# W loaded in two parts behind the first rows, block 0 loaded in four parts, the first store behind chunk 15

## The chip, the cores and the metric

The kernel runs on one core of a Trainium2 chip. The metric is the device time of one execution in microseconds (us). A core has the engines PE (TensorE, the matrix products), DVE (VectorE), ACT (ScalarE), POOL (GpSimd) and SP (SyncE, which here only issues transfers and waits), and 16 DMA engines that move data between HBM, the memory outside the core, and SBUF, the memory inside it. PE writes its results to PSUM, and another engine copies them from there. Engines run on their own and wait for each other by semaphores.

## The reference

```python
W_adapted = W + scale * (lora_A @ lora_B)
W_norm = np.sqrt(np.sum(W_adapted ** 2, axis=0, keepdims=True) + 1e-8)
W_final = W_adapted / W_norm * m
y = x.reshape(-1, 256) @ W_final          # x: 16 x 2048 x 256, float32
```

W is 256 x 256, lora_A 256 x 16, lora_B 16 x 256, m 256 numbers, scale 1. x has 32,768 rows of 256 numbers, which are 33.55 MB; y is as large. W is 0.26 MB.

## The kernel before

The 32,768 rows are cut into 8 blocks of 4096 rows (`NBLK`, `BLK`); each block is one SBUF buffer of 128 partitions x 32 rows, 32 KB in a partition. A block has 8 chunks (`CH`), and a chunk is 4 rows of each partition, 4 KB in a partition. Two chunks are a pair; there are 64 chunks (`NCH`) and 32 pairs (`NPR`). Five block buffers (`XBUFS`) are there for 8 blocks. Results are written over the rows that they come from, and stored from the same buffer. So a load of block 5, 6 or 7 has to wait until the store of block 0, 1 or 2 has landed (lines 148 to 152).

SP issues the loads in the order of the list `loads` (lines 110 and 111): first all of W, then block 0 in two parts (chunks 0 and 1, then the six others), blocks 1 to 6 whole, block 7 in two halves. ACT issues lora_A, lora_B and m at its start (lines 143 to 147), and the stores later, between its copies. SP's transfers are queue q1 in the profile, ACT's are q10.

The weights are made first. PE transposes lora_A (L248) and multiplies it by lora_B (L252); DVE adds W (L198, the only one that waits for W) and squares (L202); PE sums the squares over the partitions (L259) and spreads m (L264); ACT takes the root (L227); DVE multiplies by m, inverts the norm, and scales (L207 to L213), which gives `w_final`.

Then comes the stream over the pairs. POOL rounds a pair of chunks to bf16 (L176, `xb`); the first of these also waits for DVE's squares (line 173), and POOL waits for a load only where a pair is the first one of it (line 168). PE transposes the pair (L278, `xt_ps`), DVE copies that to SBUF (L217, `xt`), PE multiplies it by `w_final` (L292, `y_ps`, one half of the pair after the other), ACT copies each chunk's result into the block buffer (L234) and issues the stores. PE's order is written out by hand: the transposes of pair 0, a wait for `w_final` (line 303), and then a loop whose body is: transposes of pair p + 1, product of pair p. The product of a pair thus stands behind the transposes of the next one.

When a store is issued is set by one line and a constant, `HOLD`, 13 before:

```python
issue = [max(g0 + cnt - 1, HOLD + n) for n, (g0, cnt) in enumerate(stores)]   # line 117
```

Store n goes out behind ACT's copy of chunk `issue[n]`. With 13 these are chunk 13 for block 0 (its own last chunk is 7), chunk 15 for block 1, chunk 23 for block 2, and from there on each block's last chunk. The last block is stored in two halves.

At the end SP waits for the last stores and clears their semaphores (lines 315 to 317).

Of the kernel before, what the change touches and what calls it, by code (L numbers as in the profile page):

```python
# [11 lines left out]
def kernel(  # L12
# [10 lines left out]
    nc = tc.nc  # L23
    P = 128
# [10 lines left out]
    KC = IN // P  # L35
# [3 lines left out]
    NBLK = N // BLK  # L39
# [4 lines left out]
    CH = DJ // J  # L44
# [2 lines left out]
    NPR = NCH // 2  # L47
    PRB = CH // 2
    NXB = 2
    HOLD = 13  # L50
    IDLE = 8
    NXT = 2
    F8 = 2 * J * P
# [8 lines left out]
    def sb(name, shape, dtype):  # L62
        return ctx.enter_context(nc.sbuf_tensor(name, shape, dtype))
# [7 lines left out]
    w_nat = sb("w_nat", [P, KC, OUT], FP32)  # L71
# [30 lines left out]
    def sem(name):  # L102
        if name not in sems:
            sems[name] = tc.alloc_semaphore(name)
        return sems[name]
# [1 line left out]

    loads = [(0, 2), (2, CH - 2)] + [(b * CH, CH) for b in range(1, NBLK - 1)]  # L110
    loads += [(NCH - CH, CH // 2), (NCH - CH // 2, CH // 2)]
    load_of = {g: n for n, (g0, cnt) in enumerate(loads) for g in range(g0, g0 + cnt)}
    stores = [(b * CH, CH) for b in range(NBLK - 1)]
# [2 lines left out]

    issue = [max(g0 + cnt - 1, HOLD + n) for n, (g0, cnt) in enumerate(stores)]

    def in_sbuf(g0, cnt):
        b, c = divmod(g0, CH)  # L120
        return x_bufs[b % XBUFS][:, c * J : (c + cnt) * J, :]

    def in_dram(dram, g0, cnt):
        if g0 + cnt <= CH:
            block = dram[0:BLK].rearrange("(p j) k -> p j k", p=P)
            return block[:, g0 * J : (g0 + cnt) * J, :]
        return dram[g0 * J * P : (g0 + cnt) * J * P].rearrange("(p j) k -> p j k", p=P)

    def load_x(n):
        nc.sync.dma_start(  # L130
            out=in_sbuf(*loads[n]), in_=in_dram(x_flat, *loads[n])
        ).then_inc(sem(f"load{n}"), 16)

    def store_y(n):
# [2 lines left out]
        ).then_inc(sem(f"store{n}"), 16)  # L137


    nc.sync.dma_start(  # L140
        out=w_nat[:], in_=W.rearrange("(p t) o -> p t o", t=KC)
    ).then_inc(sem("load_w"), 16)
    nc.scalar.dma_start(
        out=a_nat[:], in_=lora_A.rearrange("(p t) r -> p t r", t=KC)
    ).then_inc(sem("load_a"), 16)
    nc.scalar.dma_start(out=b_nat[:], in_=lora_B).then_inc(sem("load_b"), 16)
    nc.scalar.dma_start(out=m_row[:], in_=m[None, :]).then_inc(sem("load_m"), 16)
    for n in range(len(loads)):
        b = loads[n][0] // CH
        if b >= XBUFS and loads[n][0] % CH == 0:  # L150
            nc.sync.wait_ge(sem(f"store{b - XBUFS}"), 16)
        load_x(n)


    nc.gpsimd.memset(zeros[:], 0.0).then_inc(sem("pool"), 1)
# [2 lines left out]
        out=identity[:],  # L158
        in_=zeros[:],
# [5 lines left out]
    ).then_inc(sem("ident"), 1)  # L165
    for p in range(NPR):
        b, c = divmod(p, PRB)
        if p == 0 or load_of[2 * p - 1] != load_of[2 * p]:
            nc.gpsimd.wait_ge(sem(f"load{load_of[2 * p]}"), 16)
        if p == 0:  # L170


            nc.gpsimd.wait_ge(sem("dve"), 4)
        if p >= NXB:
            nc.gpsimd.wait_ge(sem("turned"), p - NXB + 1)
        nc.gpsimd.tensor_copy(  # L176
            out=xb_bufs[p % NXB][:],
            in_=x_bufs[b % XBUFS][:, 2 * c * J : 2 * (c + 1) * J, :],
        ).then_inc(sem("rounded"), 1)
# [5 lines left out]
    for _ in range(IDLE):  # L185
# [7 lines left out]
    nc.vector.tensor_copy(out=b_bf[:], in_=b_nat[:])  # L193
    nc.vector.wait_ge(sem("pe"), 1)
    nc.vector.tensor_copy(out=aT[:], in_=aT_ps).then_inc(dv, 1)  # L195
    nc.vector.wait_ge(sem("load_w"), 16)
    nc.vector.wait_ge(sem("pe"), 2)
    nc.vector.scalar_tensor_tensor(  # L198
        out=wa[:], in0=ab_ps, scalar=float(scale), in1=w_nat[:], op0=ALU.mult, op1=ALU.add
# [15 lines left out]
    for p in range(NPR):  # L215
        nc.vector.wait_ge(sem("turned"), p + 1)
        nc.vector.tensor_copy(  # L217
            out=xt_bufs[p % NXT][:].rearrange("p r t -> p (r t)").bitcast(FP32),
            in_=xt_ps[p % 2][:],
# [8 lines left out]
        out=norm[:], in_=n2_ps, func=AF.Sqrt, bias=eps_col[:]  # L228
    ).then_inc(sem("act"), 1)
    for g in range(NCH):  # L230
        b, c = divmod(g, CH)
# [3 lines left out]
            out=x_bufs[b % XBUFS][:, c * J : (c + 1) * J, :], in_=y_ps[g % 2][:]  # L235
# [117 lines left out]
```

## Time and profile before

| What | Value |
|---|---|
| Median of 9 runs | 163.63 us (163.34 to 164.21) |
| Profiled execution | 163.4 us, of which the span from first to last instruction is 162.1 us |
| Bytes moved | 67.42 MB, mean 416 GB/s |
| PE busy | 102.4 us (63%) |
| W: issue to landing | 2.8 us, 256 KB |
| First part of block 0: issue to landing | 5.4 us, 1024 KB |
| Second part of block 0 | 12.2 us, 3072 KB |
| SP's last instruction | starts at 162.1 us |

The profile is one execution. Its span leaves out what the device does before the first and after the last instruction, here 1.3 us. Busy time of an engine is the time in which it executes instructions; the DMA share of a window is the mean over the 16 DMA engines, and GB/s is what they moved there. In a timeline a row gives the start in us, the length in us, the engine, the line, the operation and what it writes and reads; the bracket at its end tells how long the engine had been idle and what released it. A load or store that is issued at a time only joins a queue then; "to landing" counts from that issue, so it holds the time in the queue too. The trace also has each transfer's completion events, up to sixteen, one for each DMA engine that took part, and the packets with their start, length, size and queue, but not the number of the DMA engine.

### The profile page before, as it was taken

To read this page: it belongs to the slowest core of one execution; us is meant where nothing else is said; L and a number is where in the kernel's file an instruction comes from. 1 tells how busy PE (TensorE), PEld (TensorE's weight loads), DVE (VectorE), ACT (ScalarE), POOL (GpSimd) and SP (SyncE) were. 2 spreads that over 40 slices of the span, in tenths; PEclk is the share of its full clock that TensorE was granted. 3 is DMA by queue.
4 is the path that set the end of the run, shared out by engine and by line. 5 is a ranking of instruction groups with operands and counts; after the bars stand their busy time and mean duration, and the time that the engine had idled before them with its cause. 6 is when DMAs were issued, how large, how long until landed. Compare 5 with 4: busy or idle time off the path is not lost. (4 is left out here: it accounts for less than half of the span.)

```text
span 162.1 us, 1995 instructions
## 1 busy us (share of the span) xinstructions
PE 102.4 (63%) x786; PEld 89.2 (55%) x786; DVE 46.6 (29%) x44; ACT 64.0 (40%) x67; POOL 63.1 (39%) x39
## 2 busy tenths in 40 slices
PE   0391799999999960899400599506995920598000
PEld 0160689999999950789300589406894910486000
DVE  0429614535363530323300134302333410050000
ACT  3010047686868670058500058600585440058000
POOL 1045728677676403931000952019426300940000
PEclk9999999999999999579955589985799997599855
DMA  4999999999999999999999999999999999999996
GB/s 151 460 437 449 404 477 412 429 461 404 364 412 437 437 420 437 420 437 388 356 485 404 412 477 404 406 445 425 425 477 416 416 429 445 404 477 412 396 431 259
DMA packets 3060, 67.42 MB, mean 416 GB/s; under 512 B 481, under 2 KB 498, under 8 KB 626
## 3 DMA queue, kind: packets, MB, share of 16 engines
q1 hardware_dynamic: 1584, 33.82, 49.7%
q10 hardware_dynamic: 1474, 33.59, 48.4%
q14 instruction: 2, 0.02, 0.0%
HBM read 33.85 MB, written 33.55 MB: 416 GB/s over the span
## 5 line engine op out<-in xcount | busy, mean ns | idle before, releaser
L234 ACT COPY x_sb<-y_ps 128x1024 f32<-128x1024 f32 x64 | 62.1, 1014 | 77.8 <-PE y_ps L292 77.7
L176 POOL CAST xb<-x_sb 128x2048 bf16<-128x2048 f32 x32 | 60.6, 1904 | 79.1 <-DMA x_sb<-in_x_dram 56.8
L292 PE MATMUL y_ps<-w_final,xt 128*128 128x256 bf16 x512 | 67.6, 290 | 0.0
L278 PE MATMUL xt_ps<-identity,xb 128*128 128x128 f32 x264 | 40.3, 303 | 40.1 <-PEq L267 40.1
L217 DVE COPY xt<-xt_ps 128x1024 f32<-128x1024 f32 x32 | 39.2, 1225 | 90.5 <-PE xt_ps L278 90.5
L292 PEld LDWEIGHTS y_ps<-w_final,xt 128*128 128x128 bf16 x512 | 53.6, 105 | 8.5
L278 PEld LDWEIGHTS xt_ps<-identity,xb 128*128 128x128 f32 x264 | 34.6, 158 | 42.8 <-issue 42.4
L248 PE MATMUL y_ps<-identity,a_nat 128*16 128x128 f32 x2 | 0.6, 394 | 4.0 <-DMA a_nat<-in_lora_A_dram 4.0
L259 PE MATMUL y_ps<-sq,ones 128*128 128x256 f32 x4 | 2.1, 674 | 1.6 <-DVE sq L202 1.6
L227 ACT ACTIVATE norm<-y_ps,eps_col 128x256 f32<-128x256 f32 x1 | 0.5, 473 | 6.0 <-PE y_ps L259 6.0
L213 DVE TENSOR_TENSOR w_final<-wam,rnorm 128x256 bf16<-128x256 f32 x2 | 2.5, 1268 | 0.0
L259 PEld LDWEIGHTS y_ps<-sq,ones 128*128 128x128 f32 x4 | 1.2, 323 | 2.2 <-DVE sq L202 2.1
L248 PEld LDWEIGHTS y_ps<-identity,a_nat 128*16 128x16 f32 x2 | 0.1, 88 | 4.0 <-issue 4.0
L225 ACT ACT_TABLE_LOAD x1 | 1.3, 1283 | 2.4 <-issue 2.4
L182 POOL MEMSET xb<- 128x2048 bf16 x1 | 1.8, 1804 | 0.3 <-PE xt_ps L278 0.3
L210 DVE RECIPROCAL rnorm<-norm 128x256 f32<-128x256 f32 x1 | 1.7, 1745 | 0.0
L204 DVE COPY m_all<-y_ps 128x256 f32<-128x256 f32 x1 | 0.4, 425 | 3.3 <-PE y_ps L264 3.3
L193 DVE CAST b_bf<-b_nat 16x256 bf16<-16x256 f32 x1 | 0.3, 280 | 3.7 <-DMA b_nat<-in_lora_B_dram 3.7
L264 PE MATMUL y_ps<-m_row,ones 1*128 1x256 f32 x2 | 1.2, 710 | 0.0
L252 PE MATMUL y_ps<-b_bf,aT 16*128 16x256 bf16 x2 | 0.6, 400 | 1.0 <-DVE aT L195 1.0
L252 PEld LDWEIGHTS y_ps<-b_bf,aT 16*128 16x128 bf16 x2 | 0.1, 106 | 1.5 <-DVE aT L195 1.5
L198 DVE SCALAR_TENSOR_TENSOR wa<-y_ps,w_nat 128x512 f32<-128x512 f32 x1 | 0.7, 691 | 0.8 <-PE y_ps L252 0.8
(13 smaller groups left out, 3.7 us busy)
## 6 DMA issues: line engine op xcount, KB each, us to landing
out_dram<-x_sb ACTq DMA_DIRECT2D x7, 4096.0 KB, 34.2
x_sb<-in_x_dram SPq DMA_DIRECT2D x6, 4096.0 KB, 29.3
x_sb<-in_x_dram SPq DMA_DIRECT2D x2, 2048.0 KB, 30.2
out_dram<-x_sb ACTq DMA_DIRECT2D x2, 2048.0 KB, 11.9
x_sb<-in_x_dram SPq DMA_DIRECT2D x1, 3072.0 KB, 12.2
x_sb<-in_x_dram SPq DMA_DIRECT2D x1, 1024.0 KB, 5.4
w_nat<-in_W_dram SPq DMA_DIRECT2D x1, 256.0 KB, 2.8
a_nat<-in_lora_A_dram ACTq DMA_DIRECT2D x1, 16.0 KB, 3.0
```

The source lines that it names most:

```text
L176: nc.gpsimd.tensor_copy(out=xb_bufs[p % NXB][:], in_=x_bufs[b % XBUFS][:, 2 * c * J : 2 * (c + 1) * J, :],).then_inc(sem("rounded"), 1)
L182: nc.gpsimd.memset(xb_bufs[NPR % NXB][:], 0.0).then_inc(sem("rounded"), 1)
L198: nc.vector.scalar_tensor_tensor(out=wa[:], in0=ab_ps, scalar=float(scale), in1=w_nat[:], op0=ALU.mult, op1=ALU.add).then_inc(dv, 1)
L210: nc.vector.reciprocal(out=rnorm[:], in_=norm[:]).then_inc(dv, 1)
L213: i = nc.vector.tensor_mul(out=w_final[:, t], in0=wam[:, t], in1=rnorm[:])
L217: nc.vector.tensor_copy(out=xt_bufs[p % NXT][:].rearrange("p r t -> p (r t)").bitcast(FP32), in_=xt_ps[p % 2][:],).then_inc(sem("copied"), 1)
L225: nc.scalar.activation(out=warm[:], in_=eps_col[:], func=AF.Sqrt)
L234: nc.scalar.copy(out=x_bufs[b % XBUFS][:, c * J : (c + 1) * J, :], in_=y_ps[g % 2][:]).then_inc(sem("room"), 1)
L259: i = nc.tensor.matmul(n2_ps, ones[:], sq[:, t, :], start=(t == 0), stop=(t == KC - 1))
L264: nc.tensor.matmul(mb_ps, ones[0:1, :], m_row[:], start=True, stop=True).then_inc(pe, 1)
L278: i = nc.tensor.transpose(xt_ps[p % 2][:, j * P : (j + 1) * P], xb_bufs[p % NXB][:, j, :].bitcast(FP32), identity[:],)
L292: i = nc.tensor.matmul(y_ps[h][:, j, :], xt_bufs[p % NXT][:, r : r + P, t], w_final[:, t, :], start=(t == 0 and (j % (J // 2)) == 0), stop ...
```

## The change

Four things change together.

- The load of W moves on SP behind the first part of x, and is cut by partitions: 0 to 124 on SP's queue, and 125 to 127 on ACT's queue, between lora_B and m. Both count on the semaphore `load_w`, and the wait in front of L198 is for 32 instead of 16.
- Block 0 is loaded in four parts, of 1, 1, 2 and 4 chunks, instead of two, of 2 and 6 chunks.
- POOL looks for a new load at both chunks of a pair, so that pair 0 waits for two loads.
- `HOLD` becomes 15: the first store goes out behind chunk 15, the second behind chunk 16; the others stay where they are.

```diff
-    HOLD = 13
+    HOLD = 15
...
-    loads = [(0, 2), (2, CH - 2)] + [(b * CH, CH) for b in range(1, NBLK - 1)]
+    loads = [(0, 1), (1, 1), (2, 2), (4, CH - 4)] + [(b * CH, CH) for b in range(1, NBLK - 1)]
...
-    nc.sync.dma_start(
-        out=w_nat[:], in_=W.rearrange("(p t) o -> p t o", t=KC)
-    ).then_inc(sem("load_w"), 16)
+
+    W_CUT = 125
+
+    def load_w(engine, p0, p1):
+        engine.dma_start(
+            out=w_nat[p0:p1], in_=W.rearrange("(p t) o -> p t o", t=KC)[p0:p1]
+        ).then_inc(sem("load_w"), 16)
+
     nc.scalar.dma_start(
         out=a_nat[:], in_=lora_A.rearrange("(p t) r -> p t r", t=KC)
     ).then_inc(sem("load_a"), 16)
     nc.scalar.dma_start(out=b_nat[:], in_=lora_B).then_inc(sem("load_b"), 16)
+    load_w(nc.scalar, W_CUT, P)
     nc.scalar.dma_start(out=m_row[:], in_=m[None, :]).then_inc(sem("load_m"), 16)
     for n in range(len(loads)):
...
         load_x(n)
+        if n == 0:
+            load_w(nc.sync, 0, W_CUT)
...
-        if p == 0 or load_of[2 * p - 1] != load_of[2 * p]:
-            nc.gpsimd.wait_ge(sem(f"load{load_of[2 * p]}"), 16)
+        for g in (2 * p, 2 * p + 1):
+            if g == 0 or load_of[g - 1] != load_of[g]:
+                nc.gpsimd.wait_ge(sem(f"load{load_of[g]}"), 16)
...
-    nc.vector.wait_ge(sem("load_w"), 16)
+    nc.vector.wait_ge(sem("load_w"), 32)
```

## The prediction

> **What bounds the kernel now.** I read the page first (DMA rows, queues, chain), then the windows by stage, then the timeline of the first 53 us, then the waits of SyncE's queue, and last the completion events of each transfer in the trace, one for every DMA engine taking part.
>
> ```profile
> span 162.1 us, 1995 instructions
> ...
> PE 102.4 (63%) x786; PEld 89.2 (55%) x786; DVE 46.6 (29%) x44; ACT 64.0 (40%) x67; POOL 63.1 (39%) x39
> ...
> DMA  4999999999999999999999999999999999999996
> ...
> q1 hardware_dynamic: 1584, 33.82, 49.7%
> q10 hardware_dynamic: 1474, 33.59, 48.4%
> ...
> PE 5%; ACT 1%; ACTq 1%; issue 0%
> ```
>
> No compute engine is busy over 63%; the two queues (q1 the loads, q10 the stores) fill 49.7 + 48.4 = 98.1% of sixteen engines' span. The chain of waits explains only 7% and ends at the last store's issue, so it isn't the bound. The end is when the last DMA engine has moved its share.
>
> ```profile
> 24.00:40.00 16.00, 16.00 (x149) 14.89 (x147) 7.63 (x7) 11.57 (x12) 11.71 (x7) 1.00 1.00 432
> 40.00:45.00 5.00, 5.00 (x48) 4.65 (x47) 2.21 (x3) 3.85 (x4) 3.48 (x3) 1.00 0.97 341
> 45.00:60.00 15.00, 14.50 (x133) 13.20 (x131) 7.04 (x6) 10.98 (x12) 7.36 (x4) 1.00 1.01 435
> ...
> 75.00:79.00 4.00, 3.73 (x35) 3.19 (x32) 1.85 (x2) 3.04 (x4) 0.00 (x0) 1.00 1.07 369
> ...
> 156.00:162.10 6.10, 0.00 (x0) 0.00 (x0) 0.00 (x0) 0.00 (x0) 0.00 (x0) 0.50 0.71 304
> ```
>
> These are windows; the last two columns are DMA share and GB/s. Loads alone run at 432, loads and stores together at 435, so mixing costs nothing by itself. Three windows are poorer: at the first store (5 x (1 - 341/432) = 1.05 us lost), around 77 us (4 x (1 - 369/435) = 0.6 us), and the end, where engines finish one by one. The last store's sixteen completions: six at 160.40 to 160.52, four at 160.86 to 161.10, six at 161.48 to 162.05; mean 161.06. A perfectly even finish would be worth 162.05 - 161.06 = 1.0 us.
>
> ```profile
> 14.10 4.07 POOL L176 CAST xb<-x_sb 128x2048 bf16<-128x2048 f32 x2 [4.34 <-DMA x_sb<-in_x_dram]
> ...
> 23.83 1.89 POOL L176 CAST xb<-x_sb 128x2048 bf16<-128x2048 f32 x1 [2.85 <-DMA x_sb<-in_x_dram]
> ...
> 39.74 0.37 ACTq L135 DMA_DIRECT2D out_dram<-x_sb  x1
> ...
> 42.36 0.37 ACTq L135 DMA_DIRECT2D out_dram<-x_sb  x1
> ...
> 52.84 0.34 ACTq L135 DMA_DIRECT2D out_dram<-x_sb  x1
> ```
>
> ```profile
> SPq L130 <- DMA out_dram<-x_sb: 94.9, 3, 59.0
> ```
>
> The first of these is from the timeline: pair 1 and pair 4 wait for loads, and stores 0, 1 and 2 are issued. The second is from SyncE's waits: three loads wait for stores to give their buffers back.
>
> **What the Trainium skill says.** Page "DMA: Bandwidth & Descriptors", section "Why a DMA increments its semaphore by 16 and not by 1": a transfer from SyncE or ScalarE runs on k engines, the largest k up to 16 that divides the slowest dimension, on the lowest-numbered k, and the issuer adds 16 - k at once. So 128 partitions take 16 engines, 125 take 5, 3 take 3. The trace agrees for one row: m_row shows two update events only (2.46 and 5.18 us), all others sixteen; no run yet shows 125. Same page, "Queues, rings and completion order": an engine takes turns between the queues it has work for; the equal q1 and q10 shares agree. Same page, "Issuing engines are not separate DMA queues": all queues share the sixteen engines, so moving a transfer from SyncE to ScalarE buys no bandwidth; 98.1% together agrees.
>
> **Part 1, W by 125 and 3.** A W packet (2 KB, one partition) took 84 ns undisturbed in the trace. Before: 8 on each engine = 0.67 us. After, by the skill's rule: engines 0 to 4 carry 25 = 2.10 us, 0 to 2 one more = 2.18; engines 5 to 15 none. So engines 0 to 2 gain 1.51 us of work, 3 and 4 gain 1.43, eleven lose 0.67. The split of every x transfer is fixed at 8 packets an engine, and with backlog in a queue nothing evens the difference out later: it stands at the end.
>
> W comes later. On engine 0: first packet 1.96, chunk 0 (eight packets of 4 KB; from 8 KB at 309 and 16 KB at 611 ns I estimate 160 each = 1.28), a's eight of 13 ns, W's 2.10, some small ones 0.2, and 0.35 from last packet to completion: 6.0 us. L198 started at 6.32, after PE's product; at worst it moves by some tenths. Behind it stand the rest of the weight chain and the first cast (7.87); what hides this is the fixed transfer of x, and pair 4's wait for block 1 below. ScalarE's queue gets one more issue (0.4 to 0.5 us, rows a and b) ahead of m_row; m_row is wanted by PE at 9.79 and landed at 5.18, 4.6 us spare.
>
> **Part 2, block 0 in four parts.** Per engine 8 x (2 x 160 + 309 + 611) = 9.92 us instead of 8 x (309 + 912) = 9.77, and two more 9 ns completion writes: +0.17 us on every engine. This is on the path. SyncE issues two more DMAs at 0.44 us, so block 1 is issued at about 3.1 instead of 2.2; block 0 holds the engines to 13, so this is hidden. The pair 1 cast no longer waits for the whole block (14.10): chunks 2 and 3 are there by about 10. It gains nothing: PE waits for w_final (ends 16.41) ahead of the second transposition. The extra GpSimd waits are for loads that come first anyway; queued behind them are only casts. Block 1 completes at 23.00 to 23.75 before, later by 1.68 on engines 0 to 2, some 24.8; pair 4's cast goes from 23.83 to about 24.9, and compute is 1.0 us late until block 4's load stops it at 63.34 as before. No DMA waits for it.
>
> **Part 3, first store behind chunk 15.** Stores 0 and 1 go out behind chunks 15 and 16 instead of 13 and 15: 42.36 + 1.0 = 43.4 and 44.7; store 2 at 53.9. Meanwhile loads have both halves of the bandwidth: the five free blocks are 21.0 MB, at 432 GB/s 48.5 us, so alone they reach to 50.5. The first store packet came 4.4 us after its issue (44.1 against 39.74); after 43.4 that's 47.8, with 2.7 us spare. So the engines stay fed. Load 4 ends some 3 us earlier; store 0 then has the engines to itself and lands about 62.4 against 63.47; load 5 follows it. It is an exchange of order: the bytes are the same. The transition at 40 to 45 happens once either way; I take zero for the change of its 1.05 us, with bounds -1.05 (gone) and +0.6 (a second one like that at 77).
>
> **Sum, by engine.** Engines 5 to 15: end - 0.67 + 0.17 = -0.50, so the latest possible is 162.05 - 0.50 = 161.55. Engines 0 to 4: own end + 1.60 to 1.68. Everything hangs on where they finished. For engine 0 the trace tells it: m_row runs on it alone, and its packets, followed back to back, belong to the early six (last packet 160.07, completion about 160.40). It ends at 160.42 + 1.68 = 162.10. If 1 to 4 are early too, the end is 162.10, and I add 0.05 because the latest of five counts. Span 162.15, +0.1 on 162.05. The profiled execution took 163.4 (1.3 us outside the span) and so would take 163.5; it lies 0.23 below the median 163.63, so the median goes to 163.7.
>
> **The cases.** What this measurement can tell from no change is about 0.2%, 0.33 us.
>
> A (0.36): engines 0 to 4 are early ones; the late finish passes from one group to the other. 163.7, own range 163.3 to 164.0. For it: engine 0's place, and that the first six finish within 0.12 us of each other, like neighbours. Against it: four of the five can't be identified.
>
> B, slower (0.33): at least one of engines 1 to 4 is a middle or late one, and now carries 1.6 us more. Middle: 160.96 + 1.65 = 162.6, +0.55; late: 161.74 + 1.65 = 163.4, +1.35; taken together 164.5. It decides from an old completion of 160.8 on (160.8 + 1.6 = 162.4, +0.33). For it: ten of sixteen lie there. Against it: engine 0 doesn't.
>
> C, faster (0.25): the early engines take the load and the losses at 42 or 77 us shrink, because the first store now comes after block 3's last read (43.2) rather than across it. If the finish becomes even, 161.06 + 0.17 = 161.23, -0.8; half of the 1.05 alone is -0.5. Taken: 163.0. Against it: nothing at 45 to 60 says a later mixture is better.
>
> D (0.06): the change doesn't do what it says, the first store comes so late that loads run dry, or W delays the first product. The 2.7 us spare must be used up; +1, 164.6.
>
> Faster comes from C and a little of A: 0.28. Same is most of A: 0.32. Slower is B, D and A's upper edge: 0.40. The range 162.8 to 164.9 takes in C's and B's centres and leaves about 2 in 10 out.
>
> **What would show it.** W: five completion events at about 6 us for the large part; engines 5 to 15 silent. Last store: a group at 162 and the rest under 161.6 (A), a straggler over 162.4 (B), or all under 161.7 (C). Pair 4's cast near 24.9; first stores near 43.4 and 44.7; the windows at the first store and around 77 us at 341 and 369 GB/s or better. If the DMA share falls below 0.9 between 40 and 66, part 3's cover was wrong. If W shows sixteen completions, the step on five engines falls, and only +0.17 remains.

## The result: 1.3% slower, and the DMA engines end less evenly

| | Before | After |
|---|---|---|
| Median | 163.72 us (163.17 to 164.61, 31 runs) | 165.88 us (165.69 to 166.5, 10 runs) |
| Ratio to before | | 1.0132, 95% interval 1.0114 to 1.015 |
| Profiled execution, span | 163.4, 162.1 us | 166.03, 164.7 us |
| Last store's sixteen completions, mean | 161.06 us | 161.06 us |
| The last of them | 162.05 us | 164.68 us |

The last two rows show where the time stands at the end. The sixteen DMA engines finish on average at the same time as before; the last of them finishes 2.63 us later, and the span grew by 2.6 us.

The page of the changed kernel, those lines that answer to the ones shown of before:

```profile
span 164.7 us, 1999 instructions
...
PE 102.0 (62%) x786; PEld 88.5 (54%) x786; DVE 45.1 (27%) x44; ACT 64.1 (39%) x67; POOL 62.6 (38%) x39
...
DMA  3999999989999899998999999999999999999981
...
q1 hardware_dynamic: 1858, 33.81, 48.9%
q10 hardware_dynamic: 1480, 33.60, 47.4%
...
PE 5%; ACT 1%; ACTq 1%; issue 0%
```

The compute engines are as busy as before. The two queues still carry 33.8 and 33.6 MB, but fill 96.3% of sixteen engines' span instead of 98.1%. Where most of the missing share lies, the DMA row shows: after the first slice its digits stay at 8 or 9 until the last slice, which has 1 where before had 6.

Windows of the changed kernel (the last two columns are DMA share and GB/s):

```profile
40.00:45.00 5.00, 5.00 (x48) 4.64 (x47) 2.45 (x2) 3.62 (x4) 4.07 (x3) 1.00 0.97 419
75.00:79.00 4.00, 4.00 (x39) 3.78 (x37) 1.32 (x2) 3.31 (x4) 0.59 (x1) 1.00 1.03 442
156.00:160.50 4.50, 0.00 (x0) 0.00 (x0) 0.00 (x0) 0.00 (x0) 0.00 (x0) 0.50 0.86 366
160.50:162.50 2.00, 0.00 (x0) 0.00 (x0) 0.00 (x0) 0.00 (x0) 0.00 (x0) 0.50 0.27 115
162.50:164.70 2.20, 0.00 (x0) 0.00 (x0) 0.00 (x0) 0.00 (x0) 0.00 (x0) 0.50 0.04 15
```

In the last 4.2 us a quarter and then a twenty-fifth of the engines' capacity is in use. The two slow stretches of before, at 40 to 45 us and at 75 to 79 us, are gone in this execution (419 and 442 GB/s against 341 and 369), and still it is the slower kernel.

The completion events of the last store, in us from the start of the span, from the traces:

```
before  160.40 160.41 160.42 160.44 160.49 160.52 160.86 160.93 160.97 161.10 161.48 161.61 161.74 161.78 161.79 162.05
after   159.88 159.90 160.00 160.08 160.10 160.12 160.17 160.19 160.23 160.25 160.45 162.36 162.43 163.02 163.10 164.68
```

After, eleven engines end within 0.6 us of each other, mean 160.12. Then nothing for 1.9 us, and then five, mean 163.12. Such a group of five behind eleven stands at the loads of blocks 1 to 4 too, and at every store: block 1's load completes on eleven engines at 24.32 to 24.93 and on five at 26.66 to 26.90 (before: all sixteen at 23.00 to 23.75). Only the loads of blocks 5 to 7, which were issued after a store had landed, don't show it: block 5's completes at 88.49 to 89.18 on all sixteen.

That the mean at the end is the same is a coincidence of two differences. The first is lost time at the start, on all engines and not on five. At block 1's load the mean of the sixteen is 25.26 us, against 23.30 before, and even the eleven engines without W's 125 partitions, which have less to carry than before, stand at 24.56. The first packets of x were slow: those of 4 KB took 220 ns on average with a median of 159, those of 8 KB 376 ns on average (316 before).

The second difference makes up for it later. Add up, over all packets of 32 KB after 27 us, the time that each took beyond 1.213 us: this loss is 2.13 us for each engine before, most of it in the two slow stretches, and 0.23 us in the changed kernel. In each of the thirteen traces of this case, the mean at block 1, this loss, and 135.57 to 135.67 us more give the mean of the last store's completions. So both kinds of lost time stand at the end, and 23.30 + 2.13 happens to be nearly 25.26 + 0.23. What is left between the two executions is how far the last engine is behind the mean: 0.99 us before, 3.62 us after.

Timelines of the changed kernel, GpSimd's casts and ScalarE's first store issues:

```profile
12.34 1.89 POOL L185 CAST xb<-x_sb 128x2048 bf16<-128x2048 f32 x1 [0.15 <-DMA x_sb<-in_x_dram]
...
26.95 3.73 POOL L185 CAST xb<-x_sb 128x2048 bf16<-128x2048 f32 x2 [5.08 <-DMA x_sb<-in_x_dram]
```

```profile
43.48 0.38 ACTq L135 DMA_DIRECT2D out_dram<-x_sb  x1
...
45.19 0.37 ACTq L135 DMA_DIRECT2D out_dram<-x_sb  x1
...
54.23 0.34 ACTq L135 DMA_DIRECT2D out_dram<-x_sb  x1
```

Pair 1 no longer waits for the whole block (12.34 instead of 14.10), but pair 4 waits for the five late engines of block 1's load: 26.95 instead of 23.83. A cast can only start when the last engine of a load has landed, so every load is as late as its slowest engine. The stores leave 3.7, 2.8 and 1.4 us later than before, but no DMA engine is idle for it: by the packets' times, sixteen are under way at every moment from 8 to 156 us. SyncE waits in all as long as before (94.9 us) for the stores that three loads need:

```profile
SPq L130 <- DMA out_dram<-x_sb: 95.1, 3, 60.3
```

### The profile page after: what moved, and what is told of

Same layout as the page of the kernel before. It is cut to its first block, busy times and chain, and to the rows that moved or that the text cites. A ratio compares the mean times of both kernels' runs of the same rounds, so it can differ in the third digit from the quotient of the medians.

```text
span 164.7 us, 1999 instructions
## 1 busy us (share of the span) xinstructions
PE 102.0 (62%) x786; PEld 88.5 (54%) x786; DVE 45.1 (27%) x44; ACT 64.1 (39%) x67; POOL 62.6 (38%) x39
## 5 line engine op out<-in xcount | busy, mean ns | idle before, releaser
L287 PEld LDWEIGHTS xt_ps<-identity,xb 128*128 128x128 f32 x264 | 34.1, 157 | 42.1 <-issue 41.7
L207 DVE SCALAR_TENSOR_TENSOR wa<-y_ps,w_nat 128x512 f32<-128x512 f32 x1 | 0.7, 692 | 1.4 <-DMA w_nat<-in_W_dram 1.4
L216 DVE TENSOR_TENSOR wam<-wa,m_all 128x256 f32<-128x256 f32 x2 | 0.9, 507 | 0.0
```

Of the source, the lines that this page charges most:

```text
L216: i = nc.vector.tensor_mul(out=wam[:, t], in0=wa[:, t], in1=m_all[:])
L287: i = nc.tensor.transpose(xt_ps[p % 2][:, j * P : (j + 1) * P], xb_bufs[p % NXB][:, j, :].bitcast(FP32), identity[:],)
```

## The experiments

Three theories stood after the result. U: W's 125 partitions run on five of sixteen engines, and nothing evens that out before the end. H: the later first store costs the time. P: the four parts of block 0 cost it. Each change below is given against the changed kernel or the kernel before, as named.

### W whole, in the changed kernel

```diff
-    load_w(nc.scalar, W_CUT, P)
...
-            load_w(nc.sync, 0, W_CUT)
+            load_w(nc.sync, 0, P)
...
-    nc.vector.wait_ge(sem("load_w"), 32)
+    nc.vector.wait_ge(sem("load_w"), 16)
```

> The changed kernel with W in one transfer of 128 partitions, still behind the first chunk of rows; the rest of the change stays. Theory U (uneven W: the 125 partitions run on 5 of the 16 DMA engines, which then end 2 us and more behind the other eleven): the five late completions of the last store are gone, all sixteen lie between about 160.5 and 162.2 us, and the time falls from 165.9 to 163.0 to 164.0 us. Theory H (the late first store costs it) and theory P (block 0 in four parts costs it): the time stays at 165.3 us or more.

Measured: 163.62 us (before beside it 163.87), ratio 0.999, interval 0.9965 to 1.0015. The last store completes between 160.24 and 162.26, mean 161.02, with no gap and no group of five. Windows of this kernel's end and of 75 to 79 us:

```profile
75.00:79.00 4.00, 1.91 (x18) 1.47 (x15) 1.23 (x1) 2.31 (x3) 0.00 (x0) 1.00 1.02 344
...
160.50:162.30 1.80, 0.00 (x0) 0.00 (x0) 0.00 (x0) 0.00 (x0) 0.00 (x0) 0.50 0.13 55
```

U's prediction holds, and H and P, which said 165.3 or more, fall: with the late store and the four parts in place and W even, the whole loss is gone. The mean completion is that of the changed kernel (161.02 against 161.06, with 23.98 us at block 1 and a loss of 1.39 us after it); the last engine is 1.24 us behind the mean instead of 3.62. The slow stretch at 75 to 79 us is back (344). So is the first one, though the window of 40 to 45 us reads 419 GB/s: 13 load packets of 32 KB that start at 42.7 to 44.0 us take 1.41 to 1.90 us. The kernel is 2.3 us faster than the changed one with both.

### The cut alone, in the kernel before

W is cut into 125 and 3 partitions at its old place ahead of x (the same `load_w` calls, the wait for 32), and nothing else changes.

> The kernel before with nothing changed but W's load cut into 125 and 3 partitions, at its old place ahead of x. Theory U: five engines have the whole of W, 25 packets each, about 1.5 to 2.4 us more than before, the eleven others 0.7 us less: 165.0 to 166.3 us. Theories H and P: no change, 163.5 to 164.0 us.

Measured: 165.16 us, ratio 1.0085, interval 1.0054 to 1.0115. The cut alone slows the kernel before, as U said, but by 0.85% and not by 1.32%. Its mean completion is 161.68, its last 163.64. Of the 1.59 us by which this last one is later than that of before, 0.62 us is a later mean and 0.97 us a larger distance from the mean, so in this execution the unevenness at the end is not all of the loss.

### The later store alone, and the four parts alone, in the kernel before

```diff
-    HOLD = 13
+    HOLD = 15
```

> The kernel before with the first store behind chunk 15 and nothing else changed. Theory U: no loss; if the later store is what removed the slow stretches at 40 to 45 us and 75 to 79 us, these windows rise from 341 and 369 to 415 GB/s or more and the time falls by up to 1 us, to 162.7 to 163.8 us. Theory H: 165 us or more.

Measured: 163.34 us, ratio 0.9971, interval 0.9956 to 0.9985. H falls for a second time. The profiled execution took 164.49, 1.15 us above the median, so its windows don't tell where a gain comes from. They read 419 and 442 GB/s, which the expectation asked for; but a window counts a packet whole where it starts, and 22 load packets that start at 42.5 to 44.6 us take 1.40 to 2.12 us, so the first slow stretch is there. One engine completes the last store at 163.15, the fifteen others by 161.11.

```diff
-    loads = [(0, 2), (2, CH - 2)] + [(b * CH, CH) for b in range(1, NBLK - 1)]
+    loads = [(0, 1), (1, 1), (2, 2), (4, CH - 4)] + [(b * CH, CH) for b in range(1, NBLK - 1)]
```

(with the GpSimd waits for each chunk's load)

> The kernel before with block 0 loaded in four parts and nothing else changed. Theory U: the packets cost 0.17 us more on each engine, 163.6 to 164.2 us. Theory P: 165 us or more.

Measured: 163.51 us, ratio 0.9983, interval 0.9964 to 1.0002: no loss, and P falls.

### Both together, without the cut

The changed kernel with W in one transfer ahead of x.

> The changed kernel with W in one transfer of 128 partitions at its old place ahead of x; the first store behind chunk 15 and block 0 in four parts stay. Theory U (only the uneven W costs time): 163.0 to 163.7 us, no slower than either of these two alone (163.34 and 163.51). A rival (the later store and the four parts cost something only when together): 164.3 us or more.

Measured: 163.7 us, ratio 0.999, interval 0.9971 to 1.001. The rival (a loss only together) falls; that it would be no slower than either alone missed: it is some 0.2 to 0.4 us above the two, which were timed on another chip, and its interval overlaps both of theirs.

### The place of the cut W

The changed kernel, with the 125 partitions ahead of x.

> The changed kernel with the 125 partitions of W issued ahead of x instead of behind its first chunk. Theory U: the same five engines carry the same packets, so five late completions remain and the time is 164.8 to 166.0 us. Its finer form (part of the loss is that W's packets behind chunk 0 took 126 ns instead of 84, beside the other engines' x): 164.8 to 165.3 us, and W's packets at 84 ns. A rival (the place behind the first chunk is what costs): 164.0 us or less.

Measured: 165.25 us, ratio 1.0079, interval 1.0051 to 1.0108: close to the cut alone (1.0085). In the changed kernel W's 2 KB packets had a median of 126 ns; here the median is 84 ns, though the mean is 122: a few early ones take 0.33 to 0.65 us, and most of those from 4.0 us on, beside x, take 99 to 191 ns. So the time of the finer form holds, its 84 ns only in the median. The cut makes the loss, and the place behind the first chunk makes it larger. The two intervals of after and this kernel (1.0114 to 1.015, 1.0051 to 1.0108) don't overlap.

### An even cut

```diff
-    W_CUT = 125
+    W_CUT = 112
```

> The changed kernel with W cut at 112 instead of 125: 112 and 16 partitions, both on sixteen engines, 7 and 1 packets each; two transfers, two queues and the wait for 32 stay. Theory U: the load is even, 163.0 to 164.1 us as with W whole (163.62), no group of five. A rival (two transfers, the ScalarE queue or the common semaphore cost it): 165.3 us or more.

Measured: 163.69 us, ratio 0.9989, interval 0.996 to 1.0017. W's semaphore got 32 completions here, 16 for each part. Two transfers, two queues and the wait for 32 cost nothing that shows; how a cut falls on the engines is what counts. The profiled execution, 164.94 us, is 1.25 us above the median. It has no group of five, but one engine alone completes at 163.59, the fifteen others by 161.16. Its first x packets are nearly as slow as in the changed kernel (213 ns on average for 4 KB), and the mean at block 1 is 24.46. This speaks against slow first packets alone as the cause of the loss; it doesn't exclude that they are a part of it.

### Four and three engines instead of five

```diff
-    W_CUT = 125
+    W_CUT = 124
```

> The changed kernel with W cut at 124 instead of 125: 31 packets and 1 more on each of four engines. Theory U: four late completions instead of five, and each of the four carries 6 to 7 packets more than with 125, 0.5 to 0.9 us at 84 to 126 ns: 166.2 to 166.9 us if the slowest engine of the changed kernel is among the first four, 164.6 to 165.6 us if it is the fifth. A rival (a cut costs the same wherever it lies): 165.7 to 166.1 us with no group of four.

```diff
-    W_CUT = 125
+    W_CUT = 123
```

> The changed kernel with W cut at 123 instead of 125: 41 packets on each of three engines, 5 more partitions on five engines. Theory U: three engines carry 15 to 16 packets more than each of five did, 1.3 to 2.0 us at 84 to 126 ns, so the three last completions move out by that, beyond the engine that is slow at stores: 166.0 to 167.2 us. A rival (a cut costs the same wherever it lies): 165.7 to 166.1 us and no group of three.

Measured: 165.77 us (ratio 1.0112, 1.0066 to 1.0157) with 124, and 166.17 us (ratio 1.0145, 1.0108 to 1.0181) with 123. Block 1's load and the last store, on the engines that stand apart:

```
cut  packets  late at block 1's load        others, latest  late at the last store                others, latest
125  25-26    26.66 26.77 26.84 26.86 26.90  24.93           162.36 162.43 163.02 163.10 164.68    160.45
124  32       27.88 27.93 27.95 28.14        25.45           163.09 163.72 163.98 164.49 164.51    160.97
123  42       28.24 28.46 28.84              25.34           162.83 164.10 164.94 164.96           160.87
```

The groups have five, four and three engines, as the rule for the engine count says, and stand further back the more packets each carries: means 2.2, 2.7 and 3.4 us behind the others' mean. The time with 124 missed both numbers of its expectation, which lay at 166.2 or more and at 165.6 or less, and lies in the rival's range; but the rival denied the group of four, and it is there. The time with 123 lies in its range. The intervals of the ratios for 125, 124 and 123 overlap, so it is the completions that tell these cuts apart and not the times. The last store, however, has one more straggler than there are loaded engines, in the rows of 124 and 123: five with 124, four with 123. With 125 there is no sixth one, and one of the five is 1.6 us later than the next.

The extra one is most likely an engine that is slow at stores. In the packet record of every trace, 14 to 21 of the 32 KB store packets after 100 us take 1.24 to 1.32 us where nearly all others take 1.213. In the changed kernel's trace the 33 such packets of the whole run never overlap in time, as those of one engine don't, and lose 1.8 us together. A lone late engine also ended two executions above in which W was even (163.59 with the even cut, 163.15 with the later store alone), 2.4 and 2.0 us behind the next. With 124 it stands late without any of W, with 123 with one packet; with 125 it carries W. If engines are filled from the lowest number on, it is the fifth. No trace names an engine, so its number is inferred from the three counts.

### Less of W on the slow engine

The kernel before with the first store behind chunk 15, and `W_CUT = 68`.

> The kernel before with the first store behind chunk 15, and W, still ahead of x, cut into 68 and 60 partitions: 17 and 4 packets on the first four engines, 4 on the next eleven, none on the last. If the engine that is slow at stores is not among the first four (as the five late completions with only four loaded engines suggested), it is relieved by 4 packets, 0.34 us, and the four others have the room for 1.1 us more: 162.8 to 163.4 us. If it is among the first four: 164.1 to 164.8 us.

Measured: 163.7 us, ratio 0.9999, interval 0.9983 to 1.0016. It is above the expected range and below the rival's. Five late completions again (161.09, 161.12, 161.54, 161.84, 162.42) with four loaded engines; which of the five is the slow engine, the trace doesn't tell. That the slow engine isn't among the first four is supported; that relieving it by four packets pays is not: the later store alone, run beside it, took 163.32, and the two intervals overlap only a little. The run also changed more than the load of the engines: the second part of W landed at 12.09 us, and the first store left at 45.73 us instead of 40.49.

### The later store alone, once more

> The kernel before with the first store behind chunk 15, once more with more rounds, to see whether its small gain is real. Theory U says nothing against a gain: 163.2 to 163.7 us, ratio 0.996 to 0.9995. If the gain was chance: ratio 0.9995 to 1.002.

Measured: 163.32 us, ratio 0.9975, interval 0.9958 to 0.9991. Twice, then, the later store alone is faster than before, by 0.5 and 0.4 us, and it is the fastest version that was run. Windows of this execution (163.68 us):

```profile
40.00:45.00 5.00, 4.89 (x46) 4.32 (x44) 2.45 (x2) 3.59 (x5) 3.52 (x2) 1.00 0.91 321
75.00:79.00 4.00, 3.45 (x32) 2.93 (x29) 1.57 (x2) 3.31 (x4) 0.00 (x0) 1.00 1.01 377
```

Both slow stretches are there, as deep as before. Why the later store gains is left open: it is not that these stretches go.

## Why the prediction was wrong, point by point

- **What bounds the kernel**: right. The end is when the last DMA engine has moved its share; compute isn't in it. One reading under it proves less than it says: that q1 and q10 have equal shares follows from their equal bytes (33.82 and 33.59 MB) and doesn't show that an engine takes turns. The packet record of before does: from 100.67 us on, groups of packets from q10, q1 and q10 start 1.21 us apart.
- **W on five engines**: right. W's semaphore in the changed kernel got two early additions and eight completions, as many as five for 125 partitions and three for 3 make. That the difference would stand at the end was foreseen too, and the sign named for case B, a straggler over 162.4, is the one that came.
- **The step that failed** is in the sum by engine: "For engine 0 the trace tells it [...] belong to the early six", and from there "If 1 to 4 are early too, the end is 162.10". An order of finishing in one execution was taken for a property of the engines: the loaded engines were to end at 162.10, and they ended at 162.36 to 164.68. Part of the order in before seems to come from the slow stretches, which hit some engines for more than others: its first store completes within 0.7 us on all engines, its second, after the stretch at 77 us, within 3.3. In the changed kernel's execution they aren't there, and the eleven engines end together. Started from the mean of all engines instead of the early six, the same sum gives 161.06 + 1.65 = 162.7 for a loaded engine; the four loaded ones without the straggler measured 162.36 to 163.10, mean 162.73. That it fits so well is partly luck. By the sum, loaded and other engines end 1.65 + 0.50 = 2.15 us apart; they ended 162.73 - 160.12 = 2.61 us apart, and the mean stayed where it was only because a late start and the absent slow stretches cancelled.
- **The one slow engine** was missing from the sum. It was in the trace of before (the store packets of 1.24 to 1.32 us), and the place where it stood decided the rest: if it is the fifth, it was loaded with W, and it is the one that ended at 164.68, 2.0 us behind the mean of the four others. Rival B named this mechanism, "at least one of engines 1 to 4 is a middle or late one", but priced it from the late group's mean at 163.4; at the latest engine's own 162.05 + 1.65 it would have been 163.7.
- **W's packets at 84 ns**: too low. Behind the first chunk they took 116 ns on average, a median of 126; 25 x (116 - 84) is 0.8 us. W landed at 8.70 instead of 6.0, and L207 waited for it, which the cover of 0.3 us didn't hold; the row of the changed kernel's page:

```profile
L207 DVE SCALAR_TENSOR_TENSOR wa<-y_ps,w_nat 128x512 f32<-128x512 f32 x1 | 0.7, 692 | 1.4 <-DMA w_nat<-in_W_dram 1.4
```

The other engines' x packets slowed at the same time, so the group stood 2.2 us behind at block 1, near the 2.1 to 2.2 of the sum. Pair 4's cast came at 26.95, not 24.9. The late W and the late casts did not set the end, since the DMA engines had packets throughout. The time that the x packets themselves lost did count: 16 x (220 - 160) + 8 x (376 - 309) ns are 1.5 us for each engine, most of the 1.96 us by which the mean at block 1 is later, and the sum has no term for it. That the place costs something shows in the ratio, 1.0079 with the cut W ahead of x against 1.0132 behind the first chunk; by which of these effects is not separated.
- **Block 0 in four parts, +0.17 us on the path**: not seen. Alone it measured 0.9983 (0.9964 to 1.0002).
- **First store behind chunk 15, zero**: right that the engines stay fed (issued at 43.48 and 45.19, expected 43.4 and 44.7; the first store packet at 46.9, expected 47.8). Load 4 did not end 3 us earlier: its last engine completes at 65.70, against 63.29 before, and store 0 lands at 65.89 instead of 62.4, both on a late engine. The sign that was named against the supply, a DMA share under 0.9 between 40 and 66 us, appears in one window:

```profile
60.00:63.00 3.00, 0.89 (x9) 0.55 (x6) 0.41 (x1) 1.93 (x2) 0.00 (x0) 1.00 1.14 492
63.00:66.00 3.00, 0.00 (x0) 0.00 (x0) 0.00 (x0) 0.00 (x0) 0.24 (x1) 0.90 0.89 382
```

It comes from counting a packet where it starts: the share is 1.14 in the 3 us before, and the sixteen engines were all at work. The prediction was wrong on the gain: alone the later store brings 0.25 to 0.3%.
- **Case C** expected the slow stretches to shrink and the kernel to be faster for it. They vanished, and the loss on 32 KB packets fell by 1.9 us for each engine (2.13 to 0.23), more than the case hoped for. It was slower all the same, because as much had been lost before block 1 and the last engine was 3.62 us behind the mean.

## What to carry to other kernels

When the DMA engines bound a kernel, ask of a transfer not only how many bytes it has but on how many engines it runs, and add up each engine's packets: the mean can stay the same while the end moves with the latest engine. A partition count whose largest divisor up to 16 is small puts a transfer on few engines (125 on five, 124 on four, 123 on three), and a long queue of evenly split transfers behind it keeps the lag to the end. Read finishing order from several executions before building on it; from one execution, use the mean for the ordinary engines and look in the packets for an engine that is slow at one kind of transfer. And when two means agree, see whether they agree at an earlier transfer too: here they were 1.96 us apart at block 1.

## What the runs showed of the hardware

- 125, 124 and 123 partitions left five, four and three late engines at block 1. W's completion events number eight in each of these three cuts (as 5 + 3, 4 + 4 and 3 + 5 engines give), 32 with 112 and 16 partitions, and 19 with 68 and 60 (4 + 15). This is the rule of the Trainium skill, page "DMA: Bandwidth & Descriptors", section "Why a DMA increments its semaphore by 16 and not by 1"; the traces agree in every cut that was run.
- W's 2 KB packets took 84 ns, all of them, with W whole on sixteen engines behind the first chunk, and 116 ns on average on five engines in the same place, beside the others' x. With four and three engines they took 134 and 124 ns. What slows them wasn't tested.
- What seems to be one DMA engine takes 1.24 to 1.32 us for some of its 32 KB stores, in the packet records of all thirteen traces, against 1.213 for nearly all others. No load of the same size between 12 and 36 us takes more than 1.23.
- The slow stretches, read from load packets of 32 KB that take over 1.4 us instead of 1.21, come and go between kernels: both, near 43 and 77 us, in before, with W whole, with the cut alone, with both together without the cut, and in the later store's second run; the first and little of the second (22 packets and 6) in the later store's first run; only the first with the four parts alone; only the second with the even cut and with the cut W ahead of x in the changed kernel. The changed kernel and the cuts at 124, 123 and 68 have at most three such packets between 36 and 90 us. Their cause is open.
- In all thirteen traces the mean of the last store's sixteen completions is the mean at block 1's load, plus what the 32 KB packets lost against 1.213 us for each engine, plus 135.57 to 135.67 us.
